# Attention by head pairs in plain float32 on halves of the matmul array, in a one-core decoder block

## The chip, the cores and the metric

The kernel runs on one core of one Trainium2 chip. The metric is the device time of one execution in microseconds, as the median of several runs; lower is better. The core has a matmul engine (PE, with its weight loads shown apart as PEld), a vector engine (DVE), an activation engine (ACT), a general engine (POOL) and a queue engine that issues transfers (SP). Matmul results land in eight accumulator banks of 128 x 512 floats, called PSUM here; everything else lives in on-chip memory of 128 partitions or in DRAM.

## The reference

One decoder layer on x of 1024 positions by 1024 channels, float32:

```python
h = rms_norm(x, norm1_g);  proj = h @ w_in        # q | k | v | forget gate | conv in | pool in
q, k = rms_norm per head;  cum = cumsum(log_sigmoid(fg + b_f))
for start in range(0, S, 128):                     # 8 heads x 64, causal, blocks of 128 queries
    s = einsum('bqhd,bkhd->bhqk', qb, kb) * 64**-0.5
    s = s + cum[:, :, start:end, None] - cum[:, :, None, :end]
    p = softmax(where(ki <= qi, s, -1e30))
    outs.append(einsum('bhqk,bkhd->bqhd', p, vb))
conv = conformer_conv(...);  pool = multiscale_pool(...)
x = x + concat([att, conv, pool]) @ w_out
h2 = rms_norm(x, norm2_g);  up = causal_depthwise_conv(h2 @ w_up, ffn_dw_w)   # width 3
gate, val = split(up);      x = x + (silu(gate) * val) @ w_down
```

## The kernel before

The kernel goes through four parts in this order: the input projection with the convolution and pooling heads, attention, the output projection with the second norm, and the gated MLP. Almost every product is done with values split in two: `split` (L47) lets ACT round a float32 value to the reduced float of the matmul engine (F32R, the high part), and DVE or POOL subtract to get the low part. `mm3` (L51) then issues three reduced matmuls, high by high, high by low, low by high. The program states work in the order in which it should be preferred; a planner (the tile framework with its timeline model) puts each engine's instructions in order from that, from when their inputs and buffers come free, and from its own costs. So the order of the code is a priority, not the order on the engine.

Attention works on one head at a time, in stages `(h, g)`, with g a group of two query blocks of 128, in the order 3, 0, 2, 1 for each of eight heads (L592). For each head:

- `prep_pair` (L386) turns q and k of two heads into transposed form, four PE transposes to a bank. With q, the high part goes to one half of the 128 partitions of `qT` and the low part to the other half; with k, `kh` and `kl` hold high and low parts, and four transfers per bank on SP's queue copy each into the other half of the partitions too (L409). So one matmul over 128 partitions sums two products of a 64-channel head.
- `prep_head` (L471) splits v of one head into `vhl` (64 high and 64 low columns side by side) and lays the cumulated gate over all partitions (`ck`) by two matmuls with the selector `sel`, over 64 partitions (L479).
- `scores` (L485) does, for each query block and each chunk of up to 512 keys, a matmul with `kh`, one with `kl`, and for the last chunk a bf16 matmul that adds the causal mask (L497, L500). DVE adds `ck` and takes the row minimum (L502; scores are negated by the gain of q), ACT takes the exponential with row sum (L506), DVE the reciprocal (L508), and POOL multiplies the row of probabilities by it (L509).
- `values` (L512) transposes probabilities on PE (L521), three or four blocks to a bank of `psT`, splits them (ACT high, DVE low, 80 times) into `pt`, and multiplies with `vhl` (L530 to L532) into one bank of `psX`; its upper 64 partitions hold the product with v's low part, which ACT copies and DVE adds (L535, L537) into `matt`.

Scores run three stages ahead of values (`LOOK`). Filling work, `mix_work` (L575), projects the conv and pool channels through `w_out`: 16 steps `mix_out` of twelve matmuls of 512 columns each, taken from a generator at every second stage from the fifth on; it pauses until `prep_done`, since it needs a buffer that the q and k of the last pair hold. Accumulator banks in this part: two `psS` for scores, three `psT`, one `psX`, two `psF` (`fbank`, shared by `ck`, `prep_pair` and the fill).

## Time and profile before

| | |
|---|---|
| median of three runs | 1163.26 us (1162.57 to 1165.81) |
| profiled execution | 1164.96 us |
| its span, first to last instruction | 1163.1 us |
| PE busy in the span | 1107.4 us (95%) |
| DVE busy | 882.9 us (76%) |
| ACT busy | 576.1 us (50%) |
| POOL busy | 361.5 us (31%) |
| first `sel` matmul of attention (L479) | 244.3 us |
| last transpose of probabilities (L521) | 415.9 us |
| mean granted clock of PE | 0.983 |

The profile gives each instruction a start and a duration. Rows of instruction groups read: line, engine, operation, output<-inputs, shape (partitions x elements), count | busy us, mean ns | idle us of the engine ahead of them and who ended it. Rows of the timeline read: start in us, duration in us, engine, line, operation, what it writes and reads, shape, count. For matmuls the shape begins with the rows and columns of the array that are used (`128*128`, `64*128`). Matmuls overlap their neighbours, so their rate is read from the distance of starts or ends. Rows of waits read: who <- for whom, us in total, times, longest. Rows of stages list, after the stretch and its length, busy us and count for PE, PEld, DVE, ACT and POOL, then the granted clock, the transfer share and GB/s.

### The profile page before, as it was taken

To read this page: it belongs to the slowest core of one execution; us is meant where nothing else is said; L and a number is where in the kernel's file an instruction comes from. 1 tells how busy PE (TensorE), PEld (TensorE's weight loads), DVE (VectorE), ACT (ScalarE), POOL (GpSimd) and SP (SyncE) were. 2 spreads that over 40 slices of the span, in tenths; PEclk is the share of its full clock that TensorE was granted. 3 is DMA by queue.
4 is the path that set the end of the run, shared out by engine and by line. 5 is a ranking of instruction groups with operands and counts; after the bars stand their busy time and mean duration, and the time that the engine had idled before them with its cause. 6 is when DMAs were issued, how large, how long until landed. Compare 5 with 4: busy or idle time off the path is not lost.

```text
span 1163.1 us, 15556 instructions
## 1 busy us (share of the span) xinstructions
PE 1107.4 (95%) x5684; PEld 921.6 (79%) x5684; DVE 882.9 (76%) x1259; ACT 576.1 (50%) x1045; POOL 361.5 (31%) x373
## 2 busy tenths in 40 slices
PE   8999889989999999879999999999999999899996
PEld 6788889978778878658888888888888788688875
DVE  5798964758997745788877878787878656998663
ACT  7422456688998644455443545443535443233331
POOL 1365597776666652101212121212121210000010
PEclk9999999999999999979999999999999999999998
DMA  9221110023111141211312121312131397573361
GB/s 359 71 81 30 36 28 19 15 73 83 55 47 43 41 154 73 109 37 55 109 55 108 56 109 55 109 55 108 56 109 55 134 333 267 216 262 105 136 222 62
DMA packets 51885, 119.99 MB, mean 103 GB/s; under 512 B 6368, under 2 KB 11872, under 8 KB 48992
## 3 DMA queue, kind: packets, MB, share of 16 engines
q1 hardware_dynamic: 46208, 99.06, 25.7%
q0 software_dynamic: 5600, 19.93, 4.3%
q8 instruction: 45, 0.74, 0.2%
q14 instruction: 32, 0.26, 0.1%
HBM read 94.84 MB, written 19.92 MB: 99 GB/s over the span
## 4 chain that ended last, share of the span: by engine, by line
PE 71%; DVE 8%; issue 7%; DMA 5%; POOL 4%; ACT 4%; SPq 1%; POOLq 0%; ACTq 0%; DVEq 0%
PE b L55 12%; PE b L53 12%; PE b L54 12%; PE mm L53 3%; PE mm L55 3%; PE mm L54 3%; DVE acc L255 2%; PE s L497 2%; PE t L521 2%; DVE dl L49 2%; PE y L54 2%; PE y L55 1%; PE x L54 1%; PE x L55 1%; PE y L53 1%
## 5 line engine op out<-in xcount | busy, mean ns | idle before, releaser
L812 POOL TENSOR_TENSOR ac<-ac 128x1024 f32<-128x1024 f32 x22 | 61.3, 2788 | 368.7 <-ACT u L793 207.9
L768 DVE SCALAR_TENSOR_TENSOR ac<-u,par,ac 128x1023 f32<-128x1023 f32 x88 | 112.7, 1281 | 9.6 <-ACT ac L766 8.6
L53 PE MATMUL mm<-w,hh 128*128 128x256 f32 (+1 forms) x384 | 110.2, 287 | 8.6 <-DVE qk L443 4.4
L54 PE MATMUL mm<-w,hh 128*128 128x256 f32 (+1 forms) x384 | 109.3, 285 | 0.6 <-POOL w L49 0.6
L55 PE MATMUL mm<-w,hl 128*128 128x256 f32 (+1 forms) x384 | 108.8, 283 | 0.0
L48 ACT CAST wsh<-ws 128x2048 fp32r<-128x2048 f32 x22 | 42.1, 1913 | 123.3 <-PE b L54 123.0
L255 DVE SCALAR_TENSOR_TENSOR acc<-u,par,acc 128x512 f32<-128x512 f32 x120 | 93.4, 833 | 0.0
L49 DVE TENSOR_TENSOR dl<-dr,dh 128x1024 fp32r<-128x1024 f32 (+1 forms) x39 | 65.6, 1685 | 31.0 <-ACT dh L48 27.8
L509 POOL TENSOR_TENSOR p<-p,l 128x896 f32<-128x896 f32 (+3 forms) x64 | 72.5, 1147 | 44.3 <-DVE l L508 37.7
L48 ACT CAST dh<-dr 128x1024 fp32r<-128x1024 f32 (+1 forms) x39 | 54.7, 1402 | 61.1 <-PE y L55 27.3
L53 PEld LDWEIGHTS mm<-w,hh 128*128 128x128 f32 x384 | 73.0, 190 | 10.1 <-DVE fgt L431 4.9
L49 POOL TENSOR_TENSOR w<-wr,w 128x256 fp32r<-128x256 f32 (+1 forms) x56 | 64.8, 1183 | 40.9 <-ACT w L48 40.6
L54 PEld LDWEIGHTS mm<-w,hh 128*128 128x128 f32 x384 | 73.2, 191 | 1.3 <-POOL w L49 0.8
L54 PE MATMUL x<-dl,dh 128*128 128x512 f32 x176 | 70.9, 403 | 3.2 <-DVE dl L49 3.2
L862 POOL DMA_DIRECT2D out_dram<-acc x16 | 8.6, 540 | 209.4 <-DVE acc L858 208.9
L55 PEld LDWEIGHTS mm<-w,hl 128*128 128x128 f32 x384 | 73.1, 190 | 0.3
L55 PE MATMUL x<-dh,dl 128*128 128x512 f32 x176 | 70.4, 400 | 0.0
L766 ACT ACTIVATE ac<-u,par 128x1024 f32<-128x1024 f32 x44 | 50.6, 1150 | 35.8 <-DVE u L803 35.3
L48 ACT CAST dh<-res 128x1024 fp32r<-128x1024 f32 x22 | 23.1, 1052 | 84.0 <-PE y L55 54.0
L49 DVE TENSOR_TENSOR wsl<-ws,wsh 128x2048 fp32r<-128x2048 f32 x22 | 50.4, 2290 | 12.5 <-ACT wsh L48 12.5
L53 PE MATMUL x<-dh 128*128 128x512 f32 x176 | 54.0, 402 | 6.0 <-DVE acc L858 3.2
L675 DVE TENSOR_TENSOR ws<-wur 128x512 f32<-128x512 f32 x22 | 59.1, 2685 | 0.0
(308 smaller groups left out, 3395.5 us busy)
## 6 DMA issues: line engine op xcount, KB each, us to landing
wur<-in_w_up_dram SPq DMA_DIRECT2D x22, 1024.0 KB, 4.9
dr<-in_w_down_dram SPq DMA_DIRECT2D x66, 256.0 KB, 4.9
dr<-gd SPq DMA_DIRECT2D x55, 256.0 KB, 4.5
gd<-ac POOLq DMA_DIRECT2D x22, 512.0 KB, 3.0
res<-gd SPq DMA_DIRECT2D x22, 256.0 KB, 5.7
wr<-in_w_in_dram SPq DMA_DIRECT2D x40, 128.0 KB, 2.1
v<-in_x_dram SPq DMA_DIRECT2D x8, 512.0 KB, 8.4
wor<-in_w_out_dram SPq DMA_DIRECT2D x16, 256.0 KB, 3.1
```

Source lines behind the costliest of these rows:

```text
L48: nc.scalar.copy(out=dst_hi, in_=src)
L49: (lo or nc.vector).tensor_tensor(out=dst_lo, in0=src, in1=dst_hi.bitcast(F32), op=ALU.subtract)
L53: nc.tensor.matmul(ps, a_hi, b_hi, start=first, stop=False, skip_group_check=more)
L54: nc.tensor.matmul(ps, a_hi, b_lo, start=False, stop=False, skip_group_check=more)
L55: nc.tensor.matmul(ps, a_lo, b_hi, start=False, stop=last, skip_group_check=more)
L255: nc.vector.scalar_tensor_tensor(out=a, in0=u[:, c, o + j:o + j + 512], scalar=pc(PC_DW + c * CW + j), in1=a, op0=ALU.mult, op1=ALU.add)
L497: nc.tensor.matmul(ps[:, 0:c1 - c0], qT[:, i * P:(i + 1) * P], part[:, c0:c1], start=b == 0, stop=b == 1 and c1 < n)
L509: nc.gpsimd.tensor_tensor(out=pt[:, 0:n], in0=pt[:, 0:n], in1=l[:, 1:2].broadcast_to([P, n]), op=ALU.mult)
L675: nc.vector.tensor_tensor(out=out, in0=a, in1=b, op=ALU.subtract)
L766: nc.scalar.activation(out=ac, in_=us, func=AF.Copy, scale=pc(w0 + 2))
L768: nc.vector.scalar_tensor_tensor(out=ac[:, j:S], in0=us[:, 0:S - j], scalar=pc(w0 + 2 - j), in1=ac[:, j:S], op0=ALU.mult, op1=ALU.add)
L812: nc.gpsimd.tensor_tensor(out=a[:, 1], in0=a[:, 1], in1=a[:, 0], op=ALU.mult)
```

## The change

Attention goes by pairs of heads. q and k of a pair stay plain float32 (`qT`, `kT`, head 0 on partitions 0 to 63, head 1 on 64 to 127), without a low part and without the duplicating transfers. For each chunk, `scores` puts the mask matmuls of both heads first, then one float32 matmul per head over its own 64 partitions, into `psS` for the first and a new `psS2` for the second. Exponentials are not normalised: the row sums of four rows (two heads, two blocks) are inverted together, and POOL lays them over 64 columns each (`lb`). `values` copies transposed probabilities once, unsplit (ACT for head 0, DVE for head 1), multiplies them in float32 with the 64 columns of v straight from `vv`, head 0 into accumulator partitions 0 to 63 and head 1 into 64 to 127, transposes `lb` into the same bank, and DVE multiplies both into `matt`. There are 16 stages of pairs instead of 32 of heads, `LOOK` is two, `psT` has two banks, and `po` is taken from `fbank`. The fill is called at every stage from the third, twice once `prep_done` holds. The diff, cut to its core:

```diff
     def prep_pair(pr, bank):
-        for e in range(2):
-            tl.append([qkp.tile([P, S], F32R, name=n, tag=n) for n in ("qT", "kh", "kl")])
+        qkT[pr] = [qkp.tile([P, S], F32, name=n, tag=n) for n in ("qT", "kT")]
...
-                for e in range(2):
...
-                    nc.scalar.activation(out=hi[r, sl], in_=ps[r, :], func=AF.Copy, scale=gain)
-                    nc.vector.scalar_tensor_tensor(out=lo[ro, sl], in0=ps[r, :], scalar=gain,
-                                                   in1=hi[r, sl].bitcast(F32), op0=ALU.mult, op1=ALU.subtract)
-                    if src == 1:
-                        for t in (kh, kl):
-                            nc.sync.dma_start(out=t[o, sl].bitcast(F32), in_=t[r, sl].bitcast(F32))
+                nc.scalar.activation(out=qkT[pr][src][:, sl], in_=ps, func=AF.Copy,
+                                     scale=nqg if src == 0 else pc(PC_KG))
...
-    psT = pb.enter_context(tc.tile_pool(name="psT", bufs=3, space=PSUM))
-    psX = pb.enter_context(tc.tile_pool(name="psX", bufs=1, space=PSUM))
+    psS2 = pb.enter_context(tc.tile_pool(name="psS2", bufs=2, space=PSUM))
+    psT = pb.enter_context(tc.tile_pool(name="psT", bufs=2, space=PSUM))
...
+    def scores(pr, g):
+        qT, kT = qkT[pr]
+        l = bp.tile([P, 2, 4], F32, name="l", bufs=4)
+        for a, i in enumerate((2 * g, 2 * g + 1)):
+            n = (i + 1) * P
...
+            for c0 in range(0, n, 512):
...
+                if last:
+                    for e in range(2):
+                        nc.tensor.matmul(pss[e][:, w - P:w], ident_b, mask_b, start=True, stop=False,
+                                         skip_group_check=True)
+                for e, r in enumerate(rows):
+                    nc.tensor.matmul(pss[e][:, 0:w], qT[r, i * P:(i + 1) * P], kT[r, c0:c1], start=not last, stop=True,
+                                     skip_group_check=True)
+                for e in range(2):
...
+                    nc.vector.tensor_tensor_reduce(out=pts[e][:, c0:c1], in0=pss[e][:, 0:w], ...)
+            for e in range(2):
+                nc.scalar.activation(out=pts[e][:, 0:n], in_=pts[e][:, 0:n], func=AF.Exp, ...)
+        nc.vector.reciprocal(out=l[:, 1, :], in_=l[:, 0, :])
+        lb = bp.tile([P, 2, P], F32, name="lb", bufs=3)
+        nc.gpsimd.tensor_copy(out=lb.rearrange("p a (e d) -> p (a e) d", e=2),
+                              in_=l[:, 1, :, None].broadcast_to([P, 4, DH]))
+    def values(pr, g):
+        po = fbank()
+        for jj in range(g + 1):
...
+            for e in range(2):
...
+                    nc.tensor.transpose(out=ps[:, a * P:(a + 1) * P], in_=p[:, j * P:(j + 1) * P], identity=ident)
+                pt = bp.tile([P, 512], F32, name="pt", bufs=6)
+                if e == 0:
+                    nc.scalar.copy(out=pt[:, 0:n], in_=ps[:, 0:n])
+                else:
+                    nc.vector.tensor_copy(out=pt[:, 0:n], in_=ps[:, 0:n])
+            for j, lo in ((j0, 0), (j1, c)):
+                for e, r in enumerate(rows):
...
+                    nc.tensor.matmul(po[r, lo:256], v, src, start=j == 0, stop=diag and j == j1)
+        for a in range(2):
+            nc.tensor.transpose(out=po[:, 256 + a * P:256 + (a + 1) * P],
+                                in_=linv[pr, g][:, a, :], identity=ident)
+        nc.scalar.copy(out=rl, in_=po[:, 256:512])
+        nc.vector.tensor_tensor(out=matt[g // 2][:, pr, o:o + 256], in0=po[:, 0:256], in1=rl, op=ALU.mult)
...
-    stages = [(h, g) for h in range(H) for g in (3, 0, 2, 1)]
-    LOOK = 3
+    stages = [(pr, g) for pr in range(H // 2) for g in (3, 0, 2, 1)]
+    LOOK = 2
...
-        if n >= 4 and (n % 2 == 0 or prep_done[0]):
+        if n >= 2:
             next(fill, None)
+            if prep_done[0]:
+                next(fill, None)
```

## The prediction

> **What bounds the kernel now.** First the page's busy shares, then the span cut into stages.

> ```profile
> span 1163.1 us, 15556 instructions
> PE 1107.4 (95%) x5684; PEld 921.6 (79%) x5684; DVE 882.9 (76%) x1259; ACT 576.1 (50%) x1045; POOL 361.5 (31%) x373
> core 0: us, PE busy (x) PEld busy (x) DVE busy (x) ACT busy (x) POOL busy (x), PEclk, DMA share, GB/s
> 245.00:262.00 17.00, 13.86 (x66) 8.84 (x66) 11.61 (x39) 16.46 (x38) 15.20 (x16) 0.90 0.18 62
> 262.00:410.00 148.00, 145.26 (x958) 120.69 (x957) 124.72 (x358) 124.15 (x270) 95.60 (x83) 1.00 0.21 59
> 410.00:419.00 9.00, 8.89 (x54) 7.44 (x53) 4.03 (x7) 6.28 (x13) 4.44 (x4) 1.00 0.66 245
> ```

> The change lives almost wholly in the attention stage, 245 to 419 us. In its long middle part PE shows work in 145.3 of 148 us at full granted clock, while DVE and ACT stand at 84% and POOL at 65%. Busy matmul time can hide short stalls, so I look at who PE waits for between 244 and 436 us:

> ```profile
> PEld s L497 <- DVE m L502: 6.3, 11, 1.3
> PE s L497 <- DVE m L502: 3.1, 6, 1.0
> PEld t L521 <- DVE pt L49: 1.3, 3, 0.6
> PEld t L521 <- POOL p L509: 1.0, 2, 0.6
> POOL p L509 <- DVE l L508: 37.7, 24, 5.1
> ```

> The longest wait belongs to POOL, not PE. PE's weight loads lost 6.3 + 1.3 + 1.0 = 8.6 us to the other engines (the 3.1 is the same wait seen by the matmuls). So PE's own stream sets this stage; freeing DVE, ACT or POOL can return some 9 us at most. The question is what the change does to PE's stream.

> **PE: the price of a column.** Three stretches of PE's timeline:

> ```profile
> 344.59 0.40 PE L497 MATMUL s<-kl,qT 128*128 128x512 f32 x1
> ...
> 346.26 0.28 PE L530 MATMUL px<-pt,vhl 128*128 128x256 f32 x1
> 346.38 0.28 PE L531 MATMUL px<-pt,vhl 128*128 128x256 f32 x1
> 346.50 0.28 PE L530 MATMUL px<-pt,vhl 128*128 128x256 f32 x1
> ...
> 291.61 0.93 PE L397 MATMUL f<-ident,qk 128*128 128x128 f32 x7
> 292.38 0.93 PE L521 MATMUL t<-ident,p 128*128 128x128 f32 x7
> ...
> 21.24 0.39 PE L53 MATMUL s<-hh,w 128*128 128x512 f32 x1
> 21.47 0.62 PE L53 MATMUL mm<-hh,w 128*128 128x512 f32 x2
> 21.93 1.02 PE L200 MATMUL tp<-acc,ones 128*128 128x512 f32 x2
> 22.38 0.80 PE L53 MATMUL s<-hh,w 128*128 128x512 f32 x1
> ```

> Durations include a pipeline tail, so I compare ends or starts. Reduced-float (float32r) matmuls follow one another at 0.12 us for 256 columns, and 0.23 for 512 (21.24 to 21.47): 0.45 ns a column. Transposes: seven end 0.77 us after the seven before, 0.11 each. L200 is this kernel's one plain float32 product: a single 512-column matmul in the code, two instructions in the trace, ending at 22.95 where the instruction ahead ended at 22.09. That is 0.43 per instruction, 0.84 ns a column and pass, 1.68 ns for both passes: close to four times float32r.

> Columns: per head the score rows take 128 x (1+...+8) = 4,608 columns, the value products also 4,608. Before, each is done twice (kh and kl; high and low halves of pt): 8 x 2 x 4,608 = 73,728 columns x 0.45 = 33.1 us for scores, 33.1 for values. After, 8 x 4,608 = 36,864 columns x 1.68 = 61.9 us each if the heads of a pair run one after the other, 31.0 each if the halves overlap completely. These are the two ends: -4.2 us and +57.6 us for both products.

> No row of this trace has two half-array matmuls side by side. I take a value between. Rows 21.93 and 22.38 show order kept: the L53 behind L200 started early but ended 0.23 after it. The code issues head 0's two passes, then head 1's two. Passes of one head use the same half, so they follow each other; in order, only head 0's second pass can lie beside head 1's first. An isolated pair takes three pass times instead of four: scores 61.9 x 3/4 = 46.4 us. For values, four matmuls (eight passes) stand in a row: five times instead of eight, 5 x 0.215 = 1.08 us for a full group (0.215 being 256 columns), 0.86 for a diagonal one with its 128-column half; per pair 6 x 1.08 + 4 x 0.86 = 9.9, four pairs 39.6. Together 86.0 against 66.2: **+19.8 us**.

> Two more transposes per group for the reciprocals: 32 x 0.11 = **+3.5**. Masks (64) and other transposes stay.

> **PE: changing the shape of the array.** The `sel` matmul of L479 uses 64 rows already:

> ```profile
> 244.05 0.28 PE L55 MATMUL mm<-w,hl 128*128 128x256 f32 x1
> 244.26 0.72 PE L479 MATMUL f<-cumx,sel 64*128 64x512 f32 x2
> 244.91 0.50 PE L497 MATMUL s<-kh,qT 128*128 128x512 f32 x1
> 245.25 0.40 PE L497 MATMUL s<-kl,qT 128*128 128x512 f32 x1
> ```

> L55 ends at 244.33, the two L479 at 244.98: 0.65 us where two float32r matmuls of 512 columns cost 0.46, so +0.19 going in. The next full-array matmul ends at 245.41, 0.43 later, against 0.24 for the one after it: +0.19 coming out. An excursion to 64 rows costs 0.38 us. [...]

> How many excursions? For each pair: score chunks are one for row blocks 0 to 3, two for 4 to 7; the mask matmuls (full array) stand ahead of each last chunk, so the score matmuls form 12 runs, 10 where the last chunk of one block meets the first of the next. Value products form 10 runs between full-array transposes. 20 x 4 = 80 excursions x 0.38 = **+30.4**. For value products (128 rows, 64 columns) no row shows the price: between 0 and 0.38 each, 0 to 15.2; I take the L479 row as nearest. If the order breaks all score runs up, 12 + 10 per pair give 88.

> **What goes from the other engines.** Groups between 244 and 420 us:

> ```profile
> L509 POOL TENSOR_TENSOR p<-p,l 128x896 f32<-128x896 f32 (+3 forms) x64 | 72.5, 1147 | 44.3 <-DVE l L508 37.7 <-PE t L521 2.9 <-PE px L531 1.8
> L49 DVE TENSOR_TENSOR pt<-t,pt 128x512 fp32r<-128x512 f32 (+1 forms) x79 | 49.4, 632 | 9.0 <-ACT pt L48 8.6
> L48 ACT CAST pt<-t 128x512 fp32r<-128x512 f32 (+1 forms) x79 | 41.9, 544 | 6.8 <-PE px L531 4.3 <-PE t L521 1.6
> L405 DVE SCALAR_TENSOR_TENSOR kl<-f,par,kh 64x512 fp32r<-64x512 f32 x12 | 9.0, 747 | 0.5 <-ACT kh L404 0.3
> L405 DVE SCALAR_TENSOR_TENSOR qT<-f,nqg,qT 64x512 fp32r<-64x512 f32 x12 | 8.8, 749 | 1.0 <-ACT qT L404 0.7
> L404 ACT ACTIVATE kh<-f,par 64x512 fp32r<-64x512 f32 x12 | 8.2, 686 | 0.2
> L537 DVE TENSOR_TENSOR matt<-px,at 64x256 f32<-64x256 f32 x30 | 12.3, 412 | 1.6 <-ACT at L535 1.2
> L508 DVE RECIPROCAL l<-l 128x1 f32<-128x1 f32 x64 | 9.7, 157 | 9.6 <-ACT p L506 9.3
> L49 POOL TENSOR_TENSOR vhl<-v,vhl 128x512 fp32r<-128x512 f32 x8 | 10.3, 1290 | 7.1 <-ACT vhl L48 7.1
> ...
> L479 PE MATMUL f<-cumx,sel 64*128 64x512 f32 x16 | 7.7, 489 | 0.7 <-DVE kl L405 0.3 <-ACT ck L480 0.3
> L54 PE MATMUL f<-wo,ms 128*128 128x512 f32 x56 | 22.2, 396 | 0.0
> ```

> The 80 casts and 80 subtractions of pt become 40 ACT and 40 DVE copies: DVE -25, ACT -20 us. The q/k subtractions go (DVE -17.8), the halved ACT copies of prep roughly halve (-8), reciprocals fall from 64 to 16 (-7), the 32 products into matt become 16 (-6). DVE loses some 56 us, ACT some 35. POOL loses the normalisation and the vhl split, 82.8, and gains 16 copies of the broadcast reciprocals, bounded by the 512-wide 1.29 row: at most 21. With the stage growing, none of the three can be the bound. The return is what PE waited for: 0 to -9, I take **-5**. The 32 transfers that duplicate kh and kl leave SP's queue; nothing on PE waited for them, so 0; what stands behind them there, the w_out and x loads, can only come earlier.

> New waits: psT has two banks instead of three, and `po` now shares the two fbank banks with the fill products, prep and `ck`. A group's next transposes must wait for both pt copies (0.54 and 0.63 us from the rows above); scores and fill products cover it, but fills stop between the fourth fill and the release by `prep_done`. Without cover it is up to 40 groups x 0.63 = 25 us; I take **+3** (range 0 to 25). The transposed reciprocals end a value step, and whatever is queued on PE behind them waits for POOL's copy; that is issued two stages (over 20 us) ahead, so 0.

> Sum: 19.8 + 3.5 + 30.4 - 5 + 3 = **+52 us**. The profiled execution took 1164.96 us (span 1163.1, 1.9 outside it), 1.7 above the median 1163.26 of the three runs. On the median: **1215 us**. A difference under 0.3% (3.5 us) can't be told from none.

> **Rivals.** (1) No overlap: halves run one after the other. Then +57.6 + 3.5 + 30.4 - 2 = +90, **1253 us**. For it: no row shows overlap. Against it: PE visibly reshapes the array at L479, which it wouldn't need for 64 idle rows. (2) Complete overlap: passes of the two heads fully side by side: -4.2 + 3.5 + 30.4 - 2 = +28, **1191**; if in addition the 64-column products reshape nothing, +12, **1176**. [...] (3) Faster: runs of half-array matmuls come so bunched that the reshaping nearly vanishes, with complete overlap: -4.2 + 3.5 - 9 plus the excursions left, **1154** with none. It decides below (9 + 4.2 - 3.5) / 0.38 = 25 excursions. For it: POOL, DVE and ACT are freed, and matmuls of different stages may be put in a new order. Against it: L479's 16 matmuls, two to a head, show 489 ns in the mean against 396 for a full-array matmul of the same width (the group rows above): nearly every one is entered singly and pays. (4) Pairs torn apart: head 1's bank comes free later than head 0's, and other work is put between: no overlap and some 160 excursions, 57.6 + 3.5 + 61 = +122, **1285**.

> **How the numbers follow.** My forecast 0.42; no overlap 0.22; complete overlap 0.16; faster 0.12, with 0.04 more within 0.3%; torn pairs 0.04. The range 1172 to 1262 holds the first three with their unknown terms (0.80). Faster 0.12, same 0.04, slower 0.84.

> **What would show it.** Score and value matmuls as two instructions each at about 0.43 us per 512 columns; head 1's first pass starting beside head 0's second (three pass times per score pair); 0.19 us lost at each change between half-array and full-array matmuls; attention from 245 to about 470 us, PE still near 98% busy there, DVE under 60%, POOL under 40%; nothing changed before 229 us or after attention. Wrong if PE idles for psT or fbank banks, if pass times of the two heads coincide or add up, or if no step is lost at a shape change.

## The result, and the profile after

The changed kernel takes 1213.26 us (median of four runs, 1211.4 to 1214.72) against 1164.18 us before: a ratio of 1.0424, 95% interval 1.0407 to 1.0441. It is 49 us slower. The forecast was 1215 us.

The page of the changed kernel, span and busy shares:

```profile
span 1209.4 us, 15178 instructions
PE 1154.2 (95%) x5716; PEld 904.4 (75%) x5716; DVE 828.4 (68%) x1123; ACT 537.9 (44%) x965; POOL 287.0 (24%) x317
```

DVE, ACT and POOL work less, as the change says, and PE does 47 us more. The attention stage as a whole, from the first score matmul to the first matmul of the output projection (L53 on `c`), in the kernel before and then in the changed one:

```profile
245.00:424.00 179.00, 170.35 (x1089) 139.00 (x1090) 144.99 (x408) 149.58 (x325) 120.24 (x105) 0.99 0.23 70
```

```profile
244.00:473.00 229.00, 225.06 (x1152) 128.74 (x1152) 97.91 (x282) 113.67 (x250) 43.91 (x49) 0.96 0.10 33
```

The stage went from 179 to 229 us; all of the loss is there. PE works 225 of the 229 us, DVE's share fell from 81% to 43% and POOL's from 67% to 19%.

Where PE's time goes in that stage, worked out from the ends of neighbouring matmuls in the two traces: each is charged its column rate (as in the prediction's rows); what it takes above that right after a change of array shape is put to the change (up to 0.3 us); what the halved clock adds is put to the clock; the rest is put to waiting.

| us in the attention stage | before | after | difference | forecast |
|---|---|---|---|---|
| score matmuls | 33.0 | 47.4 | +14.4 | +13.3 |
| value matmuls | 33.0 | 38.6 | +5.6 | +6.5 |
| transposes of the reciprocals | 0 | 3.5 | +3.5 | +3.5 |
| changes of array shape (29, 229) | 6.3 | 37.0 | +30.7 | +30.4 |
| PE waits and other gaps | 24.0 | 9.8 | -14.2 | -2 |
| half clock | 1.4 | 7.2 | +5.8 | 0 |
| fill products that fall within the stage | 39.5 | 44.5 | +5.0 | 0 |

The last row is work moved, not added: five microseconds of fill that ran after the first output projection before. The rest (masks, other transposes) changed by less than 2 us. Where a change, the half clock and a wait meet, the line between them is a choice: other choices move these three rows of the changed kernel by 1 to 5 us (its waits come out between 5 and 10).

The row of waits holds more than waits for other engines. By the same ends, the kernel before has 103 gaps of about 0.055 us each, 5.6 us in all, most of them behind a matmul of 128 columns or a mask; the changed kernel has one. Gaps of 0.075 us and more, outside the half clock, come to 11.6 us before and 4.6 us after.

PE's timeline in the changed kernel (start, duration, engine, line, operation, output<-inputs, shape, count):

```profile
287.19 0.55 PE L518 MATMUL t<-ident,p 128*128 128x128 f32 x3
287.67 1.13 PE L488 MATMUL s<-kT,qT 64*128 64x512 f32 x4
288.73 0.28 PE L485 MATMUL s<-mask_b,ident_b 128*128 128x128 bf16 x2
288.94 0.92 PE L488 MATMUL s<-kT,qT 64*128 64x384 f32 x4
289.79 0.86 PE L532 MATMUL f<-pt,v 128*64 128x256 f32 x6
290.58 0.44 PE L535 MATMUL f<-ident,lb 128*128 128x128 f32 x2
...
291.86 0.55 PE L518 MATMUL t<-ident,p 128*128 128x128 f32 x3
292.34 1.12 PE L488 MATMUL s<-kT,qT 64*128 64x512 f32 x2
293.39 0.33 PE L518 MATMUL t<-ident,p 128*128 128x128 f32 x1
293.65 0.69 PE L488 MATMUL s<-kT,qT 64*128 64x512 f32 x1
```

At 287.67 four instructions (two heads, two passes each) take 1.13 us; at 292.34 two instructions (one head) take 1.12. So neighbouring heads overlap completely: two pass times for a pair, not three. But at 292.34 head and head are torn apart: one head, a transpose, the next head. Between 287.7 and 294 PE goes from part of the array to all of it and back at nearly every row. The weight loads sit idle there with no other engine to wait for:

```profile
PEld L485 <- issue: 21.0, 31, 1.5
PEld t L518 <- issue: 17.5, 40, 1.5
PEld f L532 <- issue: 11.5, 33, 0.8
PEld s L488 <- issue: 6.3, 29, 0.4
PEld f L532 <- DVE m L492: 3.5, 6, 0.8
```

Nearly all of the idle times in the first four rows (131 of 133) stand at a change of shape; the first wait for another engine comes fifth, with 3.5 us. They are not the price itself: they sum to 56 us where the changes cost 37, since matmuls still run meanwhile, and before masks such idle time stands in the kernel before too (7.0 us, 32 times), where the shape does not change.

Last, the start of attention, with the granted clock in the third column from the end, in the changed kernel:

```profile
245.00:250.00 5.00, 3.44 (x13) 1.41 (x12) 1.72 (x5) 2.61 (x8) 1.81 (x4) 0.96 0.20 61
250.00:260.00 10.00, 10.00 (x20) 2.96 (x17) 4.61 (x16) 6.84 (x12) 0.98 (x1) 0.50 0.06 22
260.00:270.00 10.00, 10.00 (x33) 6.14 (x32) 2.62 (x11) 5.89 (x16) 0.80 (x2) 0.50 0.00 0
270.00:280.00 10.00, 10.00 (x55) 4.93 (x56) 4.84 (x16) 6.18 (x12) 2.50 (x2) 0.99 0.16 55
```

PE is shown busy throughout and yet runs at half clock for 20.5 us. Before, the half clock lasted 3.4 us here:

```profile
250.00:255.00 5.00, 2.73 (x12) 1.33 (x11) 3.56 (x13) 4.99 (x10) 3.67 (x4) 0.90 0.00 0
255.00:260.00 5.00, 4.92 (x24) 3.53 (x25) 3.85 (x17) 4.54 (x12) 5.00 (x6) 0.76 0.32 107
```

### The profile page after: what moved, and what is told of

Same layout as the page of the kernel before. It is cut to its first block, busy times and chain, and to the rows that moved or that the text cites. A ratio compares the mean times of both kernels' runs of the same rounds, so it can differ in the third digit from the quotient of the medians.

```text
span 1209.4 us, 15178 instructions
## 1 busy us (share of the span) xinstructions
PE 1154.2 (95%) x5716; PEld 904.4 (75%) x5716; DVE 828.4 (68%) x1123; ACT 537.9 (44%) x965; POOL 287.0 (24%) x317
## 4 chain that ended last, share of the span: by engine, by line
PE 71%; DVE 11%; DMA 6%; issue 6%; POOL 3%; ACT 1%; SPq 1%; POOLq 0%; DVEq 0%; ACTq 0%
PE b L55 12%; PE b L54 12%; PE b L53 12%; PE s L488 5%; PE f L532 4%; DVE dl L49 4%; PE t L518 3%; PE mm L53 3%; PE mm L54 3%; PE mm L55 3%; DMA dr<-in_w_down_dram 2%; DVE acc L255 2%; DMA dr<-gd 2%; PE f L53 1%; PE f L55 1%
## 5 line engine op out<-in xcount | busy, mean ns | idle before, releaser
L53 PE MATMUL mm<-w,hh 128*128 128x256 f32 (+1 forms) x384 | 110.1, 287 | 8.7 <-DVE qk L432 4.6
L54 PE MATMUL mm<-w,hh 128*128 128x256 f32 (+1 forms) x384 | 109.4, 285 | 0.6 <-POOL w L49 0.6
L55 PE MATMUL mm<-w,hl 128*128 128x256 f32 (+1 forms) x384 | 108.8, 283 | 0.0
L48 ACT CAST wsh<-ws 128x2048 fp32r<-128x2048 f32 x22 | 42.1, 1913 | 123.3 <-PE b L54 123.0
L49 DVE TENSOR_TENSOR dl<-dr,dh 128x1024 fp32r<-128x1024 f32 (+1 forms) x39 | 65.6, 1683 | 29.2 <-ACT dh L48 26.1
L48 ACT CAST dh<-dr 128x1024 fp32r<-128x1024 f32 (+1 forms) x39 | 54.6, 1401 | 59.5 <-PE y L55 30.8
L53 PEld LDWEIGHTS mm<-w,hh 128*128 128x128 f32 x384 | 73.0, 190 | 10.3 <-DVE fgt L420 4.9
L49 POOL TENSOR_TENSOR w<-wr,w 128x256 fp32r<-128x256 f32 (+1 forms) x56 | 64.9, 1185 | 39.7 <-ACT w L48 39.5
L54 PEld LDWEIGHTS mm<-w,hh 128*128 128x128 f32 x384 | 73.2, 191 | 1.3 <-POOL w L49 0.8
L55 PEld LDWEIGHTS mm<-w,hl 128*128 128x128 f32 x384 | 73.1, 190 | 0.3
L488 PE MATMUL s<-kT,qT 64*128 64x512 f32 (+3 forms) x192 | 71.4, 568 | 1.6 <-DVE qk L432 1.6
L54 PE MATMUL x<-dl,dh 128*128 128x512 f32 x176 | 69.8, 396 | 1.9 <-DVE dl L49 1.9
L55 PE MATMUL x<-dh,dl 128*128 128x512 f32 x176 | 69.7, 396 | 0.0
L771 ACT ACTIVATE ac<-u,par 128x1024 f32<-128x1024 f32 x44 | 50.6, 1150 | 35.8 <-DVE u L808 35.3
L497 ACT ACTIVATE p<-p,m 128x896 f32<-128x896 f32 (+7 forms) x64 | 49.4, 772 | 36.2 <-DVE m L492 36.2
L53 PE MATMUL x<-dh 128*128 128x512 f32 x176 | 54.1, 403 | 8.2 <-DVE acc L863 7.4
L48 ACT CAST dh<-res 128x1024 fp32r<-128x1024 f32 x22 | 23.2, 1052 | 85.4 <-PE y L55 61.7
L492 DVE CUSTOM_DVE_ANT_0 p<-s,ck 128x512 f32<-128x512 f32 (+3 forms) x64 | 36.7, 589 | 33.9 <-PE s L488 29.3
```

The source lines that it names most:

```text
L48: nc.scalar.copy(out=dst_hi, in_=src)
L49: (lo or nc.vector).tensor_tensor(out=dst_lo, in0=src, in1=dst_hi.bitcast(F32), op=ALU.subtract)
L53: nc.tensor.matmul(ps, a_hi, b_hi, start=first, stop=False, skip_group_check=more)
L54: nc.tensor.matmul(ps, a_hi, b_lo, start=False, stop=False, skip_group_check=more)
L55: nc.tensor.matmul(ps, a_lo, b_hi, start=False, stop=last, skip_group_check=more)
L488: nc.tensor.matmul(pss[e][:, 0:w], qT[r, i * P:(i + 1) * P], kT[r, c0:c1], start=not last, stop=True, skip_group_check=True)
```

## The experiments

Ratios are to the kernel before on the same chip; the changed kernel stands at 1.0424.

### Do halves overlap? Both heads on one half (e2)

```diff
-    nc.tensor.matmul(pss[e][:, 0:w], qT[r, i * P:(i + 1) * P], kT[r, c0:c1], ...)
+    nc.tensor.matmul(pss[e][:, 0:w], qT[rows[0], i * P:(i + 1) * P], kT[rows[0], c0:c1], ...)
```

> The changed kernel, but head 1's score matmul reads head 0's q and k, so both heads of a pair use the same half of the array (head 1's scores are wrong); number and order of PE's instructions are those of the changed kernel. Theory (passes of the two heads really run side by side where they are neighbours): 43 score passes that started some 6 ns behind another now take their own time; the score stream goes from 47 us to the serial 62 us, so 1213 rises by 12 to 16 us, to 1225 to 1229. Rival (close starts are only how ends are modelled, halves never overlap): no change, 1213 within 3 us.

Measured: 1231.67 us, ratio 1.0572 (1.0546 to 1.0597). That is 18 us slower than the changed kernel. The same place of the program, on its timeline:

```profile
290.64 0.55 PE L518 MATMUL t<-ident,p 128*128 128x128 f32 x3
291.12 1.98 PE L488 MATMUL s<-kT,qT 64*128 64x512 f32 x4
293.03 0.29 PE L485 MATMUL s<-mask_b,ident_b 128*128 128x128 bf16 x2
293.25 1.55 PE L488 MATMUL s<-kT,qT 64*128 64x384 f32 x4
```

The four instructions that took 1.13 us now take 1.98. The score matmuls cost 61.9 us instead of 47.4, the 14.5 that were expected; some 2 us more come with a longer half clock (23.9 us instead of 20.5). The total lies 3 us above the range that was named, but far from the rival's: the overlap is real.

### Torn pairs: one buffer for both heads' scores (e3)

```diff
-    pss = [(psS if e == 0 else psS2).tile([P, 512], F32, ...) for e in range(2)]
+    both = (psS if turn[0] % 2 == 0 else psS2).tile([P, 2, 512], F32, ...)   # one buffer each, of two banks
+    turn[0] += 1
+    pss = [both[:, e] for e in range(2)]
```

> The changed kernel with the two heads' score banks in one buffer of two banks, so both heads' matmuls become ready together and the planner keeps them together: in the program's order 187 changes of array shape instead of 230, and 9 lone half-array runs of one matmul instead of 47. Theory (torn pairs cost the overlap and extra changes): score stream 47 to about 33 us, shape changes 37 to 30 us; 1213 falls by about 20, to 1190 to 1197. Rival (the joint buffer comes free only after both row minima, and PE waits for DVE instead): 1210 or more.

Measured: 1191.86 us, ratio 1.0228 (1.0209 to 1.0247): 21 us back. In the stage, score matmuls fell from 47.4 to 32.5 us, shape changes from 37.0 to 30.7; PE's waits rose only from 9.8 to 11.6, and the half clock shrank from 20.5 to 13.7 us. The pairs now stand together: 91 of 96 score passes run beside another, where 43 did. The rival, that PE would wait for both row minima, falls. Its timeline shows eight instructions of two pairs in one run:

```profile
289.28 0.28 PE L489 MATMUL s<-mask_b,ident_b 128*128 128x128 bf16 x2
289.49 1.56 PE L492 MATMUL s<-kT,qT 64*128 64x256 f32 x8
290.98 1.08 PE L536 MATMUL f<-pt,v 128*64 128x256 f32 x6
```

### What a mask between scores costs (e4), and both together (e5)

```diff
-                last = c1 == n
+                last = False
```

> The changed kernel without the 64 causal mask matmuls (left out, so future keys count in the diagonal blocks). In the program's order 163 changes of array shape instead of 230. Theory (a full-array mask between half-array scores costs two changes each): 67 changes at 0.14 to 0.2 us, 11 us, the masks' own 3.6 us, and up to 10 us of overlap where fewer pairs are torn: 1190 to 1199. Rival (shape changes cost nothing beyond the matmuls): only the masks' own time and the overlap, 1200 to 1209.

Measured: 1192.99 us, ratio 1.0242 (1.0224 to 1.0259): 20 us less. The masks' own 3.6 us are gone, shape changes cost 27.0 instead of 37.0 us (163 instead of 229), and score matmuls 39.2 instead of 47.4, since fewer pairs are torn; the half clock lasts 13.7 us here too. The time is in the expected range, but how the 20 us divide among masks, changes, overlap and clock is read from the trace alone.

With the joint buffer added:

> The changed kernel with both: the joint score buffer and no causal masks (left out, so future keys count in the diagonal blocks); 164 changes of array shape. Theory (score matmuls in pairs, fewer changes): against the joint buffer alone 23 changes less, 3.5 us, and 3.6 us of masks; 1192 falls to 1183 to 1188. Rival (either of the two already gave all there was, since DVE and ACT now end last): 1190 to 1194, as for each alone.

Measured: 1190.95 us, ratio 1.0237 (1.0215 to 1.0258): no better than either alone, which is the rival's number; the theory's 1183 to 1188 was missed. The profile shows the attention stage shorter than with the joint buffer alone (203.5 against 207.3 us), but what follows it longer (740.2 against 735.6 us). Why it is longer stays open. It may be no more than scatter: in the profiles of the kernel before and of the one with the wide selector (e1, below), which do the same work after attention, that part takes 739.1 and 734.4 us.

### Are halves worth it at all? Scores over all 128 rows (e6)

```diff
+    qkT[pr] = [... for n in ("qa", "qb", "kT")]           # q of each head, the other 64 rows zero
-    nc.tensor.matmul(pss[e][:, 0:w], qT[r, ...], kT[r, c0:c1], ...)
+    nc.tensor.matmul(pss[e][:, 0:w], qkT[pr][e][:, ...], kT[:, c0:c1], ...)
```

> The changed kernel with score matmuls over all 128 rows: q of each head padded with 64 rows of zeros, k of both heads as it is, so no score matmul uses half the array (one buffer of transposed probabilities less, 5 for 6, for want of room). 138 changes of array shape instead of 230, and no overlap of scores. Theory (each change costs 0.14 to 0.2 us, overlap is worth what the one-half run lost): score stream 47 to 62 us, +14.5; changes 37 to 21 us, -16; 1213 stays within 6 us, 1207 to 1214: halves gave the scores nothing. Rival (overlap is worth more than the changes cost): 1219 or more.

Measured: 1209.38 us, ratio 1.0396 (1.0373 to 1.0420), as the theory had it: the interval meets the changed kernel's. Score matmuls rise to 64 us (61.9 by their columns, the rest right behind masks), shape changes fall to 21.4, and, not expected, the half clock is gone: 0 us. As the changed kernel orders them, score matmuls on halves gain nothing over ones that leave half the rows at zero; part of that tie is the clock. Where the pairs stand together (e3), halves are some 18 us ahead of this kernel.

### The half clock: more fill early (e9), first pair on the full array (e14)

```diff
-        if n >= 2:
+        if n >= 0:
             next(fill, None)
```

> The changed kernel with the filling projections called from the first stage on (n >= 0 instead of n >= 2). Theory (PE is granted half its clock for 20 us at the start of attention, against 3.4 us before, because its work there is thin; full-array float32r matmuls among it bring the clock back): half-clock time falls to some 10 us, and 1213 by 3 to 6 us, to 1207 to 1210. Rival (the clock does not hang on that work, or fill only moves): 1213 within 3 us.

Measured: 1205.77 us, ratio 1.0371 (1.0341 to 1.0402). A little faster than expected, but not for the reason given: the half clock lasted 20.5 us as before. This theory of the clock falls.

```profile
250.00:260.00 10.00, 10.00 (x21) 3.07 (x18) 4.93 (x15) 7.00 (x13) 1.27 (x1) 0.52 0.12 44
260.00:270.00 10.00, 10.00 (x33) 5.95 (x31) 2.78 (x13) 5.95 (x15) 0.80 (x2) 0.50 0.00 0
```

What changed is the order: 213 shape changes instead of 229, and four microseconds less of score and value matmuls. The next kernel keeps the zero-padded q for the first pair and halves for the other three:

```diff
+    rr = slice(0, P) if pr == 0 else r
+    nc.tensor.matmul(pss[e][:, 0:w], qkT[pr][e][rr, ...], kT[rr, c0:c1], ...)
```

> The changed kernel with the first pair's scores alone over all 128 rows (q padded with zeros; one buffer of transposed probabilities less), the other three pairs on halves. Theory (the half clock at the start of attention comes from score matmuls that use half the array while there is little else; with full-array ones throughout it did not occur): the half-clock time falls from 20 us to under 4, and 1213 by 5 to 9 us, to 1204 to 1208. Rival (it is the order of work or a buffer that made the difference): half-clock time of 13 us or more, 1210 or more.

Measured: 1205.63 us, ratio 1.0357 (1.0329 to 1.0385), 7.6 us less (6.2 of it in the attention stage of the two profiles), and full clock from the start:

```profile
250.00:260.00 10.00, 10.00 (x37) 4.87 (x37) 5.36 (x20) 9.30 (x19) 1.28 (x1) 1.00 0.10 34
260.00:270.00 10.00, 10.00 (x55) 5.90 (x54) 6.64 (x25) 9.80 (x23) 3.44 (x5) 1.00 0.05 15
```

There are 16 shape changes fewer here too, 213, but the products cost some 2 us more, so that the clock is what is left to account for the gain. So the half clock comes from score matmuls that occupy half the array at the start of attention: 20.48 us with them in the changed kernel, none with the first pair over all rows. In the traces of the kernel before and of the changed one the granted clock is 1.0 or 0.5 and nothing between; the stretch at half clock here lasts 3.413 us before and 20.48, six times as long, after. In the changed kernel PE is shown busy for 10.00 of 10 us from 250 to 260, 8.84 of them with score matmuls on half the array, and the clock is 0.50.

Half-array work alone does not account for it. In the changed kernel the half clock ends at about 270.1, and from 266.37 to 269.83 PE runs transposes over the whole array; the score matmuls that follow are on halves again and run at a clock of 0.99 (270 to 280 us):

```profile
264.36 2.08 PE L488 MATMUL s<-kT,qT 64*128 64x256 f32 x4
266.37 0.90 PE L518 MATMUL t<-ident,p 128*128 128x128 f32 x3
267.06 1.06 PE L395 MATMUL f<-ident,qk 128*128 128x128 f32 x4
267.92 1.06 PE L518 MATMUL t<-ident,p 128*128 128x128 f32 x4
268.77 1.06 PE L395 MATMUL f<-ident,qk 128*128 128x128 f32 x4
269.76 1.28 PE L488 MATMUL s<-kT,qT 64*128 64x512 f32 x2
```

Whether the transposes ended it, how many of them that takes, and whether the shape changes themselves play a part, these runs do not show.

### The best of the changed kernel (e11)

Joint buffer and early fill together:

> The changed kernel with the joint score buffer and the fill from the first stage on. Theory (both worked through fewer torn pairs and shape changes, 183 now): 1191.9 falls by 2 to 6 us more, to 1186 to 1190. Rival (they repair the same tears): 1191 to 1194.

Measured: 1189.27 us, ratio 1.0216 (1.0196 to 1.0235). In the expected range, but its interval overlaps that of the joint buffer alone, so a gain over it isn't shown. Its median is the lowest of all versions of the change, and still 2.2% above the kernel before. The joint buffer together with the first pair over the whole array was not run.

### Does the kernel before hang on PE, on POOL or on DVE? (e1, e7, e10, e13)

The selector matmul over 128 rows, in the kernel before:

```diff
-    sel = const.tile([64, H], F32R, name="sel")
+    sel = const.tile([P, H], F32R, name="sel")      # and cumx [P, S]; rows 64 to 127 are zero
```

> The kernel before, with the selector matmul of the gate sums (sel, L479) widened from 64 to 128 rows by rows of zeros: the same 16 matmuls of 512 columns, none of them on half the array. Theory (reshaping the array costs PE about 0.2 us each way): the 15 excursions that the trace of before shows, 6.4 us by the ends of their matmuls, go; 1164.2 falls by 5 to 7 us, to 1157 to 1159. Rival (the 0.19 us at L479 belong to its weights, one column repeated 128 times, or lie beside other waits): no change within 3 us.

Measured: 1163.53 us, ratio 0.9989 (0.9975 to 1.0004): the rival's number. But the price was real in the records and does not belong to the weights: with the same weights, two selector matmuls over 128 rows now take 0.47 us together (244.08 to 244.55), where the 64-row ones took 0.65.

```profile
243.80 0.28 PE L55 MATMUL mm<-w,hl 128*128 128x256 f32 x1
243.92 0.63 PE L479 MATMUL f<-cumx,sel 128*128 128x512 f32 x2
```

The 6.3 us of changes are gone from the stage, and PE's waits rose from 24.0 to 28.9 us. In the kernel before, the room that was gained went into waits, as the rival's other reason has it. Without normalisation (L508, L509 left out):

> The kernel before without the reciprocals on DVE and the normalisation on POOL (L508, L509 left out, so rows are not divided by their sums): 82 us of POOL and DVE work gone, PE's stream as it is. Theory of the prediction (PE's own stream sets the attention stage, relief of other engines returns 0 to 9 us): 1155 to 1164. Rival (after the wide selector gave nothing, the chain over DVE, ACT and POOL sets it): 1154 or less.

Measured: 1162.89 us, ratio 0.9992 (0.9978 to 1.0005). POOL's busy time in the stage fell from 120 to 49 us and nothing came of it. Without the low part of the probabilities:

```diff
-            split(pt[:, 0, 0:n], pt[:, 1, 0:n], ps[:, 0:n])
+            nc.scalar.copy(out=pt[:, 0, 0:n], in_=ps[:, 0:n])     # matmuls read pt[:, 0] for pt[:, 1]
```

> The kernel before without the low part of the probabilities (the 80 subtractions of pt on DVE left out; the value matmuls for the low part read the high part instead, so PE has the same matmuls): 50 us of DVE work less in the attention stage. Theory (before, PE loses 24 us of its 179 us in attention to waits, mostly for DVE; DVE's relief in the changed kernel is what returned 14 of them): 1163.5 falls by 8 to 14 us, to 1150 to 1156. Rival (PE's own stream sets the stage): 1160 or more.

Measured: 1157.85 us, ratio 0.9946 (0.9924 to 0.9968), between the two theories. DVE lost 40 us of 145 in the stage, PE's waits fell only from 24.0 to 21.1, and the stage became 0.9 us shorter (178.1 against 179.1 us). Most of the gain stands after attention in the two profiles (731.3 against 739.1 us), where the code is the same; what brought it there is not known. And with the wide selector on top:

> The same, and the selector matmuls over 128 rows, so that PE never uses part of the array. Theory (a shape change costs PE 0.2 us and this comes through once PE no longer waits for DVE): 4 to 7 us below the kernel without the low part alone. Rival (the price stands in the records only and never in the time): the same as that kernel, within 2 us.

Measured: 1158.12 us, ratio 0.9947 (0.9928 to 0.9965): no gain. PE's waits rose again, from 21.1 to 25.0 us. No single relief of PE, POOL or DVE moves the kernel before by more than 0.6% in the median (0.8% at the end of the interval). What sets its attention stage is not settled; ACT, the busiest of the others (149.6 of 179 us), and the fixed order of instructions on each engine are left, and neither was tried. No version was found that is shown to beat the kernel before with its whole computation.

## Why the prediction was right, and where it was not

The total was right (1215 against 1213), and so were the sums of the two largest terms, the products and the shape changes. Much of that is luck: inside both terms the parts were wrong and made up for each other, and the waits, 12 us below the forecast, were offset by the half clock and the moved fill, 11 us together, for which it had no term. Step by step:

- **Price of a column and of a pass: right.** A float32 matmul is two instructions of 0.43 us for 512 columns on halves too: 292.34 above, 1.12 us with the pipeline tail.
- **Overlap: right in sum, wrong in mechanism.** The step "an isolated pair takes three pass times instead of four" failed. A pair that stands together takes two (287.67), a torn one four. 43 of 96 possible score passes and 122 of 160 value passes ran beside another, and that came out at 86.0 us in all, by chance the 86.0 of the forecast. The prediction had itself named pass times of the two heads that coincide as a sign that it is wrong. The rival of torn pairs and that of complete overlap were both there, in the same kernel. The one-half run shows the second (+18 us), the joint buffer the first (-21 us).
- **Shape changes: right in sum.** The forecast was 80 excursions of 0.38 us, 160 changes of 0.19; there were 200 changes more, at 0.20 going to 64 rows, about 0.14 coming out of them, and 0.15 in and out of 64 columns, so dearer by number and cheaper each, and 30.7 against 30.4 us is luck too. That every return to a mask or a transpose pays was an estimate from the L479 row; in the changed kernel they do, 0.11 us for the mask at 288.73 and 0.15 for the transpose at 293.39. That the 64-column products pay too was the open term; they do.
- **Waits: mis-sized.** -5 and +3 were taken; measured are -14.2 us, of which some 5.5 are the gaps of 0.055 us, which are too alike to be waits for other engines, and some 7 the longer ones. The claim behind it, that PE's own stream sets the stage before, did not hold as put: taking 6.3 us off PE gave nothing that shows (e1). The stage before had 24 us of waits and gaps, of which the idle time of PE shows 8.7 us (busy 170.35 of 179.00 us); the others hide under the pipeline tails that the durations of matmuls include (0.28 us shown for 256 columns, where the next starts 0.12 us later). The forecast that POOL's relief is worth nothing was right (e7).
- **Clock: missing.** The forecast had no term for it. The half clock's +5.8 us in the stage is borne out by the first pair on the full array (clock at 1.00, the stage 6.2 us shorter).
- **What was freed elsewhere: right.** DVE is at 43% and POOL at 19% of the stage, under the 60 and 40 that were named; PE at 98%. In the stage DVE lost 47 us of the 56 that were forecast and ACT 36 of 35, though the terms named for ACT add up to 28 only.

Complete overlap, the second rival, was given 0.16. It held wherever a pair stood together: the passes of the two heads start 6 to 7 ns apart in the trace of the changed kernel.

## What to carry to other kernels

Count how often PE alternates between whole-array and part-array matmuls before putting small products on parts of the array: at 0.11 to 0.20 us a change (changed kernel), a run of part-array matmuls must be long to be worth its two changes. By the rows here, at 0.43 us a pass of 512 columns, an overlapped pair of float32 matmuls saves some 0.86 us at 512 columns and 0.22 at 128, and an excursion to 64 rows costs 0.3 to 0.4. If two matmuls are to overlap, make them ready by the same event (one buffer for both): with a bank of its own for each head, the planner, which works by readiness, let only 43 of 96 score passes run beside another; with one buffer it was 91. And do not count on the relief of an engine before trying it: here each engine's relief, tried by leaving its work out, moved the kernel by 0.6% at most.
